# A recurrent unit's small products over four quarters of the array, its copies and elementwise steps given out anew

## The chip, the cores and the metric

The kernel runs on one core of a Trainium2 chip. The metric is device time in microseconds, the median of the runs. The engines that matter are TensorE (PE; its weight loads are PEld), VectorE (DVE), ScalarE (ACT) and GpSimd (POOL).

## The reference

One block of a network: a token mixer with two branches (softmax attention with a forget gate, and an RWKV-7 recurrence), then a gated convolutional feed-forward part. The change lies in the recurrence alone, 8 heads of 64 over 1024 tokens:

```python
def step(state, inp):
    r_t, w_t, k_t, v_t, a_t, b_t = inp
    sa = jnp.einsum('bhvk,bhk->bhv', state, a_t)
    state = state * w_t[:, :, None, :] + sa[..., None] * b_t[:, :, None, :] + v_t[..., None] * k_t[:, :, None, :]
    y_t = jnp.einsum('bhvk,bhk->bhv', state, r_t)
    return state, y_t
...
kk = heads(k * k_k)
kk = kk / jnp.maximum(jnp.sqrt(jnp.sum(kk * kk, axis=-1, keepdims=True)), L2_EPS)
k_mod = k.astype(jnp.float32) * (1 + (a - 1) * k_a)
...
mean = jnp.mean(y, axis=-1, keepdims=True)
var = jnp.mean(jnp.square(y - mean), axis=-1, keepdims=True)
y = ((y - mean) * lax.rsqrt(var + GN_EPS)).reshape(bsz, seq, RWKV_WIDTH) * ln_w + ln_b
bonus = (jnp.sum(r_h * k_h * r_k, axis=-1, keepdims=True) * v_h).reshape(bsz, seq, RWKV_WIDTH)
return ((y + bonus) * g).astype(p.dtype)
```

## The kernel before

The recurrence is computed in chunks of 64 tokens, in closed form. A *unit* is a pair of heads (`p`, four of them) and half of the tokens (`hf`), so there are eight units, numbered 0 to 7 here (`k` in the code), with eight chunks each. One head of the pair lies on partitions 0 to 63, the other on 64 to 127 (`HS[0]`, `HS[1]`).

`pre` prepares a unit. It loads two rows of `d_lora`, forms the decay (`cum`, `el`, `en`), normalises the key (`ksq`, `ssq`, `kr`) and in eight elementwise steps makes `ar` (the vectors read by), `bk` (those written with) and `rkb`, mostly on VectorE. Then come the products `p1` (`p` in the profile) of `bk` with `ar`, masked into `E`; a triangular solve of 31 steps on VectorE (`t` and `E32`, shown as `t` and `E`) on blocks that go out and back by DMA (`sm`, `M32`, `se`, `TT`); transposes `vt` and `at`, copied into `UV` and `QA`; transposes `tb`; and the product `q`.

`main` finishes a unit. VectorE transposes a quarter of `TT` into `X` (two instructions); the products `xi` and `zi` complete the inverse in `TT`. The product `uw` applies it to `QA`, and gives `Wt` and the second half of `UV`; the product `mz` of `Wt` and `E` gives `Zt` and the transition `Mt`. Both are 16 products of 64x64 by 64x128, for each chunk and head, and go into two PSUM banks of four chunks each. Head h is read from partitions `HS[h]` and written to partitions `HS[h]`. Blocks `sp` and `yp` follow, then eight steps of the state `S` (TensorE to ScalarE and back), then `y`, its mean `mu` (subtracted by the first `stt` on `y`), its variance `va` and the group norm.

Two chains, `main_chain` for unit k and `pre_chain` for the units after it, are generators. Each `yield` says how long, in the planner's nanoseconds, the chain stays away; meanwhile the planner `Weave` fills TensorE with the big products of the next projections (`qk`, `ps_rkv`, `v`, `gt`). This writes TensorE's order, which is fixed. The orders of VectorE, ScalarE, GpSimd and the queues come from a scheduler that knows the program's order and dependencies. Where `marks` holds an instruction, `add_manual_dep` without a semaphore puts another one behind it in that order: `X` stands behind the last state step `S`, the last mask `E` and, from unit 5 on, the last copy of `QA`.

Of the kernel before, what the change touches and what calls it, by code (L numbers as in the profile page):

```python
# [12 lines left out]
ALU = mybir.AluOpType  # L13
# [3 lines left out]
S = 1024  # L17
# [5 lines left out]
CH = 64  # L23
# [109 lines left out]
def hybrid_block(ctx: ExitStack, tc: tile.TileContext, a, out):  # L133
# [32 lines left out]
    def V(name, i=0, n=1):  # L166
        o, _ = VEC[name]
        return vec[:, o + i : o + i + n]
# [197 lines left out]
    with ExitStack() as es:  # L366
# [328 lines left out]
        def c3(ap):  # L695
            return ap.rearrange("p (c s) -> p c s", s=CH)
# [23 lines left out]
        def pre(k, p, hf):  # L720
# [8 lines left out]
            def chunk_tile(nm, bufs, *dims):  # L729
                return rw.tile([128, *dims], F32, tag=nm, name=f"{nm}{n}", bufs=bufs)  # L730
# [27 lines left out]
                yield 200  # L758
            ar = chunk_tile("ar", 2, 2, NCU, CH)
            stt(ar[:, 0], c3(kr), nkk[:, p : p + 1], el[:, :, 0:CH], op0=ALU.mult, op1=ALU.mult)  # L760
            stt(kr, kr, V("k_k", p), al, op0=ALU.mult, op1=ALU.mult)
            tt(bk[:, :, 0, :], c3(kr), c3(en), op=ALU.mult)
            nc.gpsimd.tensor_copy(bk[64:128, :, 2, :], bk[64:128, :, 0, :])
            tt(ar[:, 1], c3(rr), el[:, :, 1:], op=ALU.mult)
            ts(al, al, V("k_a", p), oka[:, p : p + 1], op0=ALU.mult, op1=ALU.add)
            tt(al, al, kk, op=ALU.mult)
            tt(bk[:, :, 1, :], c3(al), c3(en), op=ALU.mult)
            pcd = chunk_tile("pcd", 3, NCU)
            nc.gpsimd.tensor_copy(pcd, el[:, :, CH])
            rkb = tmp("ksq")  # L770
            stt(rkb, rr, V("r_k", p), al, op0=ALU.mult, op1=ALU.mult)
            yield 10500


            while (k - 2, 0) not in passed:
# [55 lines left out]
            for e in range(2):  # L831
                for h in range(2):
                    nc.scalar.copy(UV[HS[1 - h], e::2, h, :], v4[HS[e], :, h, :])
                    marks["QA"] = nc.vector.tensor_copy(QA[HS[h], e::2, 1, :], a4[HS[e], :, h, :])
            yield 2000
            ps = [gen(f"tb{n}{h}") for h in range(2)]
            for c in range(NCU):
# [15 lines left out]
        def main(k, p, hf):  # L853
            o = units.pop((p, hf))
            n = f"{p}_{hf}"
            cs = slice(hf * NH, hf * NH + NH)
            pcd, ar, E, QA, TT, bon, UV = (o[k] for k in ("pcd", "ar", "E", "QA", "TT", "bon", "UV"))


            X = rw.tile([128, NCU, 32], F32, tag="X", name=f"X{n}", bufs=1)  # L860
            B0 = (slice(0, 32), slice(64, 96))
            B1 = (slice(32, 64), slice(96, 128))
            yield max(0, o["ready"] - weave.now - 2500)
            for h in range(2):
                i = nc.vector.transpose(X[B0[h], :, :], TT[B0[h], :, 0:32])
                for x in ("S", "E", "bank") if k == 0 else ("S", "E", "QA") if k > 4 else ("S", "E"):
                    if x in marks:
                        tc.add_manual_dep(i.ins, marks[x].ins.name, NOSYNC)
            yield max(1300, o["ready"] - weave.now)
            xi = gen(f"xi{n}")  # L870
            for c in range(NCU):
                for h in range(2):
                    mm(xi[B1[h], c * 32 : c * 32 + 32], E[B0[h], c, h, 0, 32:64], X[B0[h], c, :], start=True, stop=True)
            for h in range(2):
                nc.scalar.copy(X[B1[h], :, :], hx(xi[B1[h], 0 : NCU * 32], 32))
            yield 2360
            zi = gen(f"zi{n}")
            for c in range(NCU):
                for h in range(2):
                    mm(zi[B0[h], c * 32 : c * 32 + 32], X[B1[h], c, :], TT[B1[h], c, 32:64], start=True, stop=True)  # L880
            for h in range(2):
                nc.scalar.copy(TT[B0[h], :, 32:64], hx(zi[B0[h], 0 : NCU * 32], 32))

            yield 2000
            Wt = rw.tile([128, NCU, CH], F32, tag="Wt", name=f"Wt{n}", bufs=1)
            for c0 in range(0, NCU, 4):
                ps = gen(f"uw{n}{c0}")
                for c in range(c0, c0 + 4):
                    for h in range(2):
                        x = (c - c0) * 128  # L890
                        mm(ps[HS[h], x : x + 128], TT[HS[h], c, :], QA[HS[h], c, :, :], start=True, stop=True)
                pv = ps.rearrange("p (c a s) -> p c a s", a=2, s=CH)
                nc.vector.tensor_copy(Wt[:, c0 : c0 + 4, :], pv[:, :, 1, :])
                for h in range(2):
                    nc.scalar.copy(UV[HS[h], c0 : c0 + 4, h, :], pv[HS[h], :, 0, :])
            yield 2970
            Zt = rw.tile([128, NCU, CH], F32, tag="Zt", name=f"Zt{n}", bufs=1)
            for c0 in range(0, NCU, 4):
                ps = gen(f"mz{n}{c0}")
                for c in range(c0, c0 + 4):  # L900
                    for h in range(2):
                        x = (c - c0) * 128
                        mm(ps[HS[h], x : x + 128], Wt[HS[h], c, :], E[HS[h], c, h, 1:3, :], start=True, stop=True)
                pv = ps.rearrange("p (c a s) -> p c a s", a=2, s=CH)
                tt(Zt[:, c0 : c0 + 4, :], pv[:, :, 0, :], ar[:, 1, c0 : c0 + 4, :], op=ALU.add)
                for h in range(2):
                    tt(Mt[HS[h], c0 : c0 + 4, HS[h]], pv[HS[h], :, 1, :],
                       ident[HS[h], HS[h]].unsqueeze(1).to_broadcast([64, 4, CH]), op=ALU.add)

            yp = py.tile([128, NCU, CH], F32, tag="yp", name=f"yp{n}")  # L910
            sp = py.tile([128, NCU, CH], F32, tag="sp", name=f"sp{n}")
            S = [state.get(p)]

            for c in range(NCU):
                for h in range(2):
                    mm(sp[HS[h], c, :], E[:, c, h, 2, :], UV[:, c, h, :], start=c == 0, stop=False, more=True)
                for h in range(2):
                    mm(yp[HS[h], c, :], UV[:, c, h, :], E[:, c, h, 1, :], start=c == 0, stop=False, more=True)
            passed.add((k, 0))
            yield 3400  # L920
            last_c = NCU - 1 - hf
            for c in range(last_c + 1):
                if S[c] is not None:
                    mm(sp[:, c, :], Mt[:, c, :], S[c], start=False, stop=c == last_c, more=True)
                S.append(rw.tile([128, CH], F32, tag="state", name=f"S{n}{c}", bufs=8))
                state_done(nc.scalar.activation(S[-1], sp[:, c, :], AF.Copy, scale=pcd[:, c : c + 1]), c == last_c)
                if c + 1 < NCU:
                    yield 1150

            for c in range(NCU):  # L930
                if S[c] is not None:
                    for h in range(2):
                        mm(yp[HS[h], c, :], S[c][HS[h], :], Zt[HS[h], c, :], start=False, stop=c == NCU - 1, more=True)
            state[p] = S[-1]
            passed.add((k, 1))

            y = rw.tile([128, NH], F32, tag="y", name=f"y{n}", bufs=1)
            nc.scalar.copy(y, yp.rearrange("p c s -> p (c s)"))

            def part(nm, i):  # L940
                return rw.tile([128, NH], F32R, tag=nm, name=f"{nm}{i}{n}", bufs=1)

            mu = gen(f"mu{n}")
            yield 700
            yield from head_sums(mu, y, part("Zt", "r"), part("Wt", "r"))
            stt(y, mu, -1.0 / CH, y, op0=ALU.mult, op1=ALU.add)
            ysq = rw.tile([128, NH], F32, tag="ysq", name=f"ysq{n}", bufs=1)
            nc.scalar.activation(ysq, y, AF.Square)
            yield 2700
            va = gen(f"va{n}")  # L950
            yield from head_sums(va, ysq, part("Zt", "s"), part("Wt", "s"))
            gg = rw.tile([128, NH], F32, tag="ysq", name=f"gg{n}", bufs=1)
            nc.sync.dma_start(gg, d_lora[2, p, :, cs])
            rs = rw.tile([128, NH], F32, tag="Zt", name=f"rs{n}", bufs=1)
            nc.scalar.activation(rs, va, AF.Ln, scale=1.0 / CH, bias=epsr[:, 1:2])
            nc.scalar.activation(rs, rs, AF.Exp, scale=-0.5)
            stt(y, y, V("ln_w", p), rs, op0=ALU.mult, op1=ALU.mult)
            stt(y, y, V("ln_b", p), bon, op0=ALU.add, op1=ALU.add)
            tt(gg, y, gg, op=ALU.mult)
            nc.sync.dma_start(d_orw[p, :, cs], gg)  # L960
# [1111 lines left out]
```

## Time and profile before

| | us |
|---|---|
| median of 3 runs | 1649.46 (1647.59 to 1650.44) |
| the profiled execution's own time | 1648.58 |
| its span in the profile | 1646.8 |
| TensorE busy | 1606.6 (98%) |
| VectorE busy | 1214.0 (74%) |
| ScalarE busy | 827.6 (50%) |

The span runs from the first to the last instruction of the program; the rest of the own time lies around it. The eight units fill about 150 to 620 us; attention, the output products and the feed-forward part follow. Busy times of TensorE overlap, since a matmul's record is longer than the distance to the next one; the distance between starts tells how long a block holds the engine.

### The profile page before, as it was taken

The page shows a single profiled execution, that of the slowest core. Times are in us where ns is not written, and L with a number is a line of the kernel's source. Part 1 is how long each engine was busy: PE and PEld are TensorE (multiplying, and loading weights), DVE is VectorE, ACT ScalarE, POOL GpSimd, SP SyncE. Part 2 cuts the span into 40 slices and gives each one's busy share as a digit, 9 for nine tenths or more (in the row PEclk, how much of TensorE's full clock was granted, in tenths as well). Part 3 has the DMA queues.
Part 4 walks back from the last instruction along what each step waited for, and adds up shares of the span by engine and source line. Part 5 has one row for each costly group of instructions (what it writes and reads, how often), then busy time and mean ns, then how long its engine had stood idle before and what let it go on. Part 6 is the DMA issues. An engine that isn't in the chain of part 4 may idle for free.

```text
span 1646.8 us, 25966 instructions
## 1 busy us (share of the span) xinstructions
PE 1606.6 (98%) x9694; PEld 1339.6 (81%) x9694; DVE 1214.0 (74%) x2345; ACT 827.6 (50%) x1557; POOL 159.2 (10%) x189
## 2 busy tenths in 40 slices
PE   7999999999999999999999999999999999999998
PEld 7777788898978788888888888788888888888886
DVE  4786787878876536888678547887777777886677
ACT  5563345444445656777623235644444444555455
POOL 0011101111111011333132000000000000000000
PEclk9999999999999999999999999999999999999999
DMA  9397645543433336434197420242232232675363
GB/s 338 121 344 229 183 130 139 137 117 94 114 103 98 97 122 163 128 106 118 50 357 264 175 80 26 84 135 96 96 120 98 96 109 96 223 256 160 122 211 109
DMA packets 121646, 240.60 MB, mean 146 GB/s; under 512 B 40048, under 2 KB 48880, under 8 KB 121520
## 3 DMA queue, kind: packets, MB, share of 16 engines
q1 hardware_dynamic: 113040, 220.58, 41.2%
q0 software_dynamic: 8480, 18.37, 4.2%
q8 instruction: 76, 1.25, 0.3%
q14 instruction: 50, 0.41, 0.1%
HBM read 173.35 MB, written 65.54 MB: 145 GB/s over the span
## 4 chain that ended last, share of the span: by engine, by line
PE 58%; DVE 5%; ACT 2%; DMA 2%; issue 1%; SPq 0%; POOL 0%; ACTq 0%; DVEq 0%; POOLq 0%
PE X L141 13%; PE D L141 13%; PE Y L141 6%; PE wo L141 5%; PE br L141 5%; PE W L141 3%; PE rk_ps L141 3%; PE gt L141 3%; PE ov L141 2%; PE lg L141 2%; PE tp L145 1%; DMA vh<-d_v 1%; DVE quads L1075 1%; DVE P L1085 1%; DVE tl L1115 0%
## 5 line engine op out<-in xcount | busy, mean ns | idle before, releaser
L141 PE MATMUL D<-op,op 128*128 128x512 f32 x924 | 209.8, 389 | 0.0
L141 PEld LDWEIGHTS D<-op,op 128*128 128x128 f32 x924 | 173.3, 188 | 36.3 <-DVE op L1295 0.3
L141 PE MATMUL X<-T_m,S 128*128 128x512 f32 x440 | 107.8, 390 | 1.7 <-ACT T_m L1756 1.1
L141 PEld LDWEIGHTS X<-T_m,S 128*128 128x128 f32 x440 | 82.4, 188 | 20.4 <-ACT T_m L1756 2.5
L1294 ACT CAST op<-g 128x512 fp32r<-128x512 f32 x77 | 47.8, 621 | 72.9 <-PE D L141 47.6
L1295 DVE TENSOR_TENSOR op<-g,op 128x512 fp32r<-128x512 f32 x77 | 53.0, 689 | 41.2 <-ACT op L1294 41.2
L1553 DVE SCALAR_TENSOR_TENSOR c<-ab,vec,c 128x512 f32<-128x512 f32 x88 | 65.9, 750 | 18.4 <-ACT c L1556 16.8
L807 DVE TENSOR_TENSOR t<-E,M 128x60 f32<-128x60 f32 (+24 forms) x248 | 55.7, 224 | 26.7 <-DMA M<-sm 20.7
L1519 DVE TENSOR_TENSOR A<-ur,A 128x512 fp32r<-128x512 f32 x64 | 44.0, 689 | 38.7 <-ACT A L1515 38.5
L1519 DVE TENSOR_TENSOR S<-ur,S 128x512 fp32r<-128x512 f32 x66 | 45.5, 691 | 35.2 <-ACT S L1515 35.0
L1515 ACT CAST S<-ur 128x512 fp32r<-128x512 f32 x66 | 41.0, 622 | 55.8 <-DVE ur L1508 30.6
L290 DVE TENSOR_TENSOR lo_in<-raw_in,hi_in 128x512 fp32r<-128x512 f32 x84 | 55.5, 701 | 15.3 <-PE gt L141 4.5
L141 PE MATMUL Y<-T_h,A 128*128 128x512 f32 x264 | 63.7, 390 | 0.3 <-ACT T_h L1756 0.3
L288 ACT CAST hi_in<-raw_in 128x1024 fp32r<-128x1024 f32 x42 | 43.9, 1050 | 40.0 <-PE qk L141 18.6
L141 PE MATMUL Y<-T_h,S 128*128 128x512 f32 x264 | 63.5, 390 | 0.4 <-ACT T_h L1774 0.4
L809 DVE TENSOR_TENSOR E<-E,t 128x60 f32<-128x60 f32 (+24 forms) x248 | 57.6, 232 | 6.3
L1115 DVE TENSOR_TENSOR tl<-tp,th 128x512 fp32r<-128x512 f32 (+1 forms) x80 | 50.0, 631 | 15.3 <-ACT th L1112 15.1
L1515 ACT CAST A<-ur 128x512 fp32r<-128x512 f32 x64 | 39.6, 621 | 42.9 <-PE X L141 31.3
L141 PE MATMUL W<-B_f,A 128*128 128x512 f32 x252 | 60.6, 389 | 0.0
L141 PE MATMUL X<-B_b,A 128*128 128x512 f32 x252 | 60.5, 389 | 0.0
L141 PEld LDWEIGHTS Y<-T_h,S 128*128 128x128 f32 x264 | 49.5, 188 | 11.0 <-ACT T_h L1774 0.8
L141 PEld LDWEIGHTS Y<-T_h,A 128*128 128x128 f32 x264 | 49.5, 188 | 11.0 <-ACT T_h L1756 0.7
(485 smaller groups left out, 4160.6 us busy)
## 6 DMA issues: line engine op xcount, KB each, us to landing
raw_in<-in_w_in SPq DMA_DIRECT2D x50, 512.0 KB, 3.7
wm<-in_w_mod SPq DMA_DIRECT2D x48, 512.0 KB, 7.4
ur<-in_w_up SPq DMA_DIRECT2D x44, 512.0 KB, 4.0
g<-d_g SPq DMA_DIRECT2D x35, 512.0 KB, 4.1
d_g<-gs SPq DMA_DIRECT2D x44, 256.0 KB, 2.1
d_g<-c SPq DMA_DIRECT2D x33, 256.0 KB, 4.5
d_st<-qh SPq DMA_DIRECT2D x64, 128.0 KB, 2.5
stA<-d_st POOLq DMA_DIRECT2D x8, 1024.0 KB, 8.1
```

What stands on the lines that cost most here:

```text
L141: nc.tensor.matmul(o, lhsT, rhs, start=start, stop=stop, skip_group_check=more)
L145: nc.tensor.transpose(o, i, eye)
L288: nc.scalar.copy(hi, raw)
L290: nc.vector.tensor_tensor(lo[:, c : c + NH], raw[:, c : c + NH], f32(hi[:, c : c + NH]), op=ALU.subtract)
L807: tt(tv, E32[:, 0:J, s : s + 1].to_broadcast([128, J, W]), M32[:, s : s + 1, s + 1 : 32].to_broadcast([128, J, W]), op=ALU.mult)
L809: tt(E32[:, 0:J, s + 1 : 32], E32[:, 0:J, s + 1 : 32], tv, op=ALU.add)
L1115: tt(tl[:, 0:w], tp[:, 0:w], f32(th[:, 0:w]), op=ALU.subtract)
L1294: nc.scalar.copy(hi, src)
L1295: tt(lo, src, f32(hi), op=ALU.subtract)
L1515: nc.scalar.copy(hi, src)
L1519: tt(lo, src, f32(hi), op=ALU.subtract)
L1553: stt(c, ab[:, x + hf * NH : x + hf * NH + NH], V("conv_w", 22 * x + i), c, op0=ALU.mult, op1=ALU.add)
```

## The change

Four things are changed.

- `uw` and `mz`: the two banks now take the even and the odd chunks. For an odd chunk head h is written to the other partition half, `HS[1 - h]`. The copies and sums that read the odd chunks take each head by itself: `Wt` and `Zt` are made by three instructions a unit each where there were two; `UV` and `Mt` keep four.
- The four copies of `at` into `QA` go from VectorE to ScalarE.
- The eight elementwise steps of `pre` were issued together, with a pause of 10500 behind them; now a pause of 800 stands between them, and one of 4900 at the end. The copy of `pcd` by GpSimd stands ahead of the last step, as before.
- For units 5 to 7, `X` stands also behind the instruction that subtracts the mean from `y` of the unit before.

```diff
--- before.py
+++ after.py
@@ pre
             stt(ar[:, 0], c3(kr), nkk[:, p : p + 1], el[:, :, 0:CH], op0=ALU.mult, op1=ALU.mult)
+            yield 800
             stt(kr, kr, V("k_k", p), al, op0=ALU.mult, op1=ALU.mult)
+            yield 800
             tt(bk[:, :, 0, :], c3(kr), c3(en), op=ALU.mult)
             nc.gpsimd.tensor_copy(bk[64:128, :, 2, :], bk[64:128, :, 0, :])
+            yield 800
             tt(ar[:, 1], c3(rr), el[:, :, 1:], op=ALU.mult)
+            yield 800
             ts(al, al, V("k_a", p), oka[:, p : p + 1], op0=ALU.mult, op1=ALU.add)
+            yield 800
             tt(al, al, kk, op=ALU.mult)
+            yield 800
             tt(bk[:, :, 1, :], c3(al), c3(en), op=ALU.mult)
+            yield 800
             pcd = chunk_tile("pcd", 3, NCU)
             nc.gpsimd.tensor_copy(pcd, el[:, :, CH])
             rkb = tmp("ksq")
             stt(rkb, rr, V("r_k", p), al, op0=ALU.mult, op1=ALU.mult)
-            yield 10500
+            yield 4900
...
                     nc.scalar.copy(UV[HS[1 - h], e::2, h, :], v4[HS[e], :, h, :])
-                    marks["QA"] = nc.vector.tensor_copy(QA[HS[h], e::2, 1, :], a4[HS[e], :, h, :])
+                    marks["QA"] = nc.scalar.copy(QA[HS[h], e::2, 1, :], a4[HS[e], :, h, :])
@@ main
-                for x in ("S", "E", "bank") if k == 0 else ("S", "E", "QA") if k > 4 else ("S", "E"):
+                for x in ("S", "E", "bank") if k == 0 else ("S", "E", "QA", "y") if k > 4 else ("S", "E"):
...
-            for c0 in range(0, NCU, 4):
-                ps = gen(f"uw{n}{c0}")
-                for c in range(c0, c0 + 4):
-                    for h in range(2):
-                        x = (c - c0) * 128
-                        mm(ps[HS[h], x : x + 128], TT[HS[h], c, :], QA[HS[h], c, :, :], start=True, stop=True)
-                pv = ps.rearrange("p (c a s) -> p c a s", a=2, s=CH)
-                nc.vector.tensor_copy(Wt[:, c0 : c0 + 4, :], pv[:, :, 1, :])
+            ps = [gen(f"uw{n}{e}") for e in range(2)]
+            for c in range(NCU):
                 for h in range(2):
-                    nc.scalar.copy(UV[HS[h], c0 : c0 + 4, h, :], pv[HS[h], :, 0, :])
+                    x = c // 2 * 128
+                    mm(ps[c % 2][HS[h ^ c % 2], x : x + 128], TT[HS[h], c, :], QA[HS[h], c, :, :], start=True, stop=True)
+            pv = [x.rearrange("p (c a s) -> p c a s", a=2, s=CH) for x in ps]
+            nc.vector.tensor_copy(Wt[:, 0::2, :], pv[0][:, :, 1, :])
+            for h in range(2):
+                nc.vector.tensor_copy(Wt[HS[h], 1::2, :], pv[1][HS[1 - h], :, 1, :])
+            for e in range(2):
+                for h in range(2):
+                    nc.scalar.copy(UV[HS[h], e::2, h, :], pv[e][HS[h ^ e], :, 0, :])
...
-            for c0 in range(0, NCU, 4):
-                ps = gen(f"mz{n}{c0}")
-                for c in range(c0, c0 + 4):
-                    for h in range(2):
-                        x = (c - c0) * 128
-                        mm(ps[HS[h], x : x + 128], Wt[HS[h], c, :], E[HS[h], c, h, 1:3, :], start=True, stop=True)
-                pv = ps.rearrange("p (c a s) -> p c a s", a=2, s=CH)
-                tt(Zt[:, c0 : c0 + 4, :], pv[:, :, 0, :], ar[:, 1, c0 : c0 + 4, :], op=ALU.add)
+            ps = [gen(f"mz{n}{e}") for e in range(2)]
+            for c in range(NCU):
                 for h in range(2):
-                    tt(Mt[HS[h], c0 : c0 + 4, HS[h]], pv[HS[h], :, 1, :],
+                    x = c // 2 * 128
+                    mm(ps[c % 2][HS[h ^ c % 2], x : x + 128], Wt[HS[h], c, :], E[HS[h], c, h, 1:3, :], start=True, stop=True)
+            pv = [x.rearrange("p (c a s) -> p c a s", a=2, s=CH) for x in ps]
+            tt(Zt[:, 0::2, :], pv[0][:, :, 0, :], ar[:, 1, 0::2, :], op=ALU.add)
+            for h in range(2):
+                tt(Zt[HS[h], 1::2, :], pv[1][HS[1 - h], :, 0, :], ar[HS[h], 1, 1::2, :], op=ALU.add)
+            for e in range(2):
+                for h in range(2):
+                    tt(Mt[HS[h], e::2, HS[h]], pv[e][HS[h ^ e], :, 1, :],
                        ident[HS[h], HS[h]].unsqueeze(1).to_broadcast([64, 4, CH]), op=ALU.add)
...
-            stt(y, mu, -1.0 / CH, y, op0=ALU.mult, op1=ALU.add)
+            marks["y"] = stt(y, mu, -1.0 / CH, y, op0=ALU.mult, op1=ALU.add)
```

The scheduled orders move with it. On TensorE, `uw` of unit 0 stood as two rows of eight, `uw_00` and `uw_04`; now pairs of `uw_00` and `uw_01` alternate. On ScalarE, what stands between unit 1's last cast and its copies of `tb` (`UV` from `vt`, `QA` from `at`) now reads:

```order
L840 COPY UV_1_1844<-vt_1_1992 64x4x64 x2
L841 COPY QA_1_1843<-at_1_1993 64x4x64 x2
L840 COPY UV_1_1844<-vt_1_1992 64x4x64
L841 COPY QA_1_1843<-at_1_1993 64x4x64
L840 COPY UV_1_1844<-vt_1_1992 64x4x64
L841 COPY QA_1_1843<-at_1_1993 64x4x64
```

Where four copies of `UV` stood alone, the four of `QA` now stand among them.

## The prediction

> **What bounds the kernel now.** I read the page's busy line first, then the sums of the stretch from 150 to 620 us, in which the eight recurrent units run and to which the whole change belongs, then TensorE's waits there.
>
> ```profile
> span 1646.8 us, 25966 instructions
> PE 1606.6 (98%) x9694; PEld 1339.6 (81%) x9694; DVE 1214.0 (74%) x2345; ACT 827.6 (50%) x1557; POOL 159.2 (10%) x189
> ...
> 150.00:620.00 470.00, 461.99 (x4226) 386.17 (x4225) 341.12 (x932) 228.04 (x431) 66.19 (x89) 1.00 0.44 125
> ```
>
> In the last row the columns are length, then busy time of TensorE, its weight loads, VectorE, ScalarE and GpSimd, then granted clock. TensorE works 462 of 470 us at clock 1.00; VectorE works 341. The waits of TensorE in that stretch (us in total, times, longest):
>
> ```profile
> PE qk L141 <- DVE ql L415: 1.9, 1, 1.9
> PE v L141 <- DVE vs L978: 1.4, 2, 0.9
> ...
> PE va L141 <- ACT Zts L712: 1.0, 1, 1.0
> PE va L141 <- POOL Wts L715: 0.9, 1, 0.9
> PE zi L141 <- ACT X L875: 0.8, 1, 0.8
> PE p L141 <- DVE bk L767: 0.4, 1, 0.4
> ```
>
> They come to a few us, so TensorE's own work sets the time, and its order is written by the planner: the big products that follow (`qk`, `ps_rkv`, `v`, `gt`) move up at once when a small product takes less. What is saved on TensorE here is saved at the end, unless another engine becomes late.
>
> **The products `uw` and `mz`.** The timeline of TensorE in unit 2 (start, us, tile, count); each product of fp32 numbers shows as two matmul records, so 16 products are x32:
>
> ```profile
> 329.56 1.96 PE L141 MATMUL uw<-QA,TT 64*64 64x128 f32 x32
> 331.45 0.74 PE L141 MATMUL v<-lo_v,u_hi 128*128 128x256 f32 x4
> ...
> 335.00 1.96 PE L141 MATMUL mz<-E,Wt 64*64 64x128 f32 x32
> 336.89 0.34 PE L141 MATMUL sp<-UV,E 128*64 128x64 f32 x4
> 337.06 0.29 PE L141 MATMUL yp<-E,UV 128*64 128x64 f32 x4
> ...
> 338.90 1.22 PE L141 MATMUL v<-hi_v,u_hi 128*128 128x256 f32 x8
> ```
>
> From start to the next start `uw` holds TensorE for 1.89 us, and so does `mz`: 0.118 us for a pair of records. Only two 64x64 quarters of the array work, the ones on the diagonal. The order of unit 1 on TensorE before (`qk` are big products):
>
> ```order
> L141 MATMUL qk_0_2824<-u_lo,hi_in_2491 128x512 x6
> L141 MATMUL uw_10_2869<-QA_1_1841,TT_1_1983 64x128 x8
> L141 MATMUL uw_14_2881<-QA_1_1841,TT_1_1983 64x128 x8
> L141 MATMUL qk_0_2824<-u_hi,lo_in_2492 128x512 x8
> L141 MATMUL qk_1_2911<-u_hi,hi_in_2491 128x512 x6
> ```
>
> Two blocks of eight, each into one bank, then the big products. Now, at the same place:
>
> ```order
> L141 MATMUL uw_10_2872<-QA_1_1843,TT_1_1985 64x128 x2
> L141 MATMUL uw_11_2873<-QA_1_1843,TT_1_1985 64x128 x2
> L141 MATMUL uw_10_2872<-QA_1_1843,TT_1_1985 64x128 x2
> L141 MATMUL uw_11_2873<-QA_1_1843,TT_1_1985 64x128 x2
> ...
> L141 MATMUL qk_0_2826<-u_hi,lo_in_2494 128x512 x7
> L141 MATMUL qk_1_2914<-u_hi,hi_in_2493 128x512 x7
> ```
>
> Even and odd chunks now alternate between two banks and, by the partitions of their outputs, between the two diagonals; 14 big products still stand between `uw` and `mz`. No row of before has all four quarters at work, so I bound it. At worst nothing overlaps: 1.89. At best the time halves: 0.95. The nearest row is the `sp`/`yp` block above: two tiles of 128 rows by 64 columns fill the array, and 64 records take from 336.89 to 338.90, 31 ns each. A quarter with 128 moving columns is half the rows and twice the columns, the same share of the array, so 32 records would take 1.00. Two row strips that write two banks also run together already, in `p`:
>
> ```profile
> 351.85 1.16 PE L141 MATMUL p<-ar,bk 64*128 64x128 f32 x16
> 352.94 0.43 PE L141 MATMUL sp<-S,Mt 128*128 128x64 f32 x2
> ```
>
> 16 records in 1.09 us, 0.136 a pair (start included). I take 1.05, one pair's 0.118 of starting up on top of the half, rounded: 0.84 saved, 16 times (two products, eight units): **-13.4 us** (bounds 0 and -15.1).
>
> The weight loads, from the groups of the same stretch (count, busy, mean ns):
>
> ```profile
> L141 PEld LDWEIGHTS p<-ar,bk 64*128 64x128 f32 x256 | 15.5, 187 | 3.9 <-issue 2.0 <-DVE bk L767 0.9 <-PE va L141 0.4
> L141 PEld LDWEIGHTS uw<-QA,TT 64*64 64x64 f32 x256 | 13.8, 133 | 2.2 <-issue 1.9
> ```
>
> A load of `p` is 54 ns longer than one of `uw`, yet a pair of `p` takes only 18 ns more, start included, so loads lie mostly under products. [...]
>
> **The elementwise work behind them.** Groups of the stretch:
>
> ```profile
> L834 DVE COPY QA<-at 64x256 f32<-64x256 f32 x32 | 13.5, 422 | 6.9 <-PE at L145 6.6
> L833 ACT COPY UV<-vt 64x256 f32<-64x256 f32 x32 | 11.7, 367 | 14.8 <-PE vt L145 14.5
> L905 DVE TENSOR_TENSOR Zt<-mz,ar 128x256 f32<-128x256 f32 x16 | 6.7, 422 | 1.0 <-PE mz L141 0.7
> L893 DVE COPY Wt<-uw 128x256 f32<-128x256 f32 x16 | 6.6, 419 | 4.8 <-PE uw L141 4.7
> ```
>
> Per unit VectorE loses four `QA` copies (1.69 us) and gains one copy for `Wt` and one sum for `Zt`, since the odd chunks' halves lie crossed (0.84): 0.85 less. I credit nothing for it, as VectorE is not the bound. ScalarE gains four copies of about 0.367, 1.5 us. Queued behind them are the copies of `tb` and the next casts; who waits first is product `q`, which reads `UV`, whose last copy is now seventh of eight. Unit 4 on ScalarE and TensorE:
>
> ```profile
> 414.45 1.50 ACT L833 COPY UV<-vt 64x256 f32<-64x256 f32 x4 [3.16 <-PE vt L145]
> ...
> 417.34 0.86 PE L141 MATMUL q<-UV,E 64*64 64x64 f32 x22
> ```
>
> `UV` would end at 415.95 + 3 x 0.367 = 417.05, still 0.3 before `q`: nothing, and at most 0.8 a unit were that cover gone.
>
> The mark that matters more is `Wt`, for which `mz` waits. VectorE's last `Wt` copy and TensorE's `mz` in units 1, 3 and 4 (the end of a copy is its start plus 0.42):
>
> ```profile
> 286.42 0.42 DVE L893 COPY Wt<-uw 128x256 f32<-128x256 f32 x1
> ...
> 287.39 0.87 PE L141 MATMUL mz<-E,Wt 64*64 64x128 f32 x12
> ...
> 381.55 0.42 DVE L893 COPY Wt<-uw 128x256 f32<-128x256 f32 x1
> ...
> 382.78 0.44 PE L141 MATMUL mz<-E,Wt 64*64 64x128 f32 x4
> ...
> 428.80 0.23 DVE L809 TENSOR_TENSOR E<-E,t 128x69 f32<-128x69 f32 x1
> 428.95 0.42 DVE L893 COPY Wt<-uw 128x256 f32<-128x256 f32 x1
> ...
> 430.34 1.96 PE L141 MATMUL mz<-E,Wt 64*64 64x128 f32 x32
> ```
>
> The margins are 0.55, 0.81 and 0.97 us. In these units VectorE runs the solve of the next unit (`t`, `E`) back to back, in a fixed order. Its order in unit 1 before:
>
> ```order
> L807 TENSOR_TENSOR t_0_2560<-E_0_2558,M_0_2553 128x68
> L893 COPY Wt_1_2868<-uw_10_2869 128x256
> L809 TENSOR_TENSOR E_0_2558<-E_0_2558,t_0_2560 128x4x17
> L807 TENSOR_TENSOR t_0_2560<-E_0_2558,M_0_2553 128x64
> L809 TENSOR_TENSOR E_0_2558<-E_0_2558,t_0_2560 128x4x16
> L893 COPY Wt_1_2868<-uw_14_2881 128x256
> ```
>
> Each copy followed its bank, two solve steps apart. Now, at the same place:
>
> ```order
> L814 TENSOR_TENSOR t_0_2563<-E_0_2561,M_0_2556 128x68
> L816 TENSOR_TENSOR E_0_2561<-E_0_2561,t_0_2563 128x4x17
> L814 TENSOR_TENSOR t_0_2563<-E_0_2561,M_0_2556 128x64
> L899 COPY Wt_1_2871<-uw_10_2872 128x4x64
> L816 TENSOR_TENSOR E_0_2561<-E_0_2561,t_0_2563 128x4x16
> L901 COPY Wt_1_2871<-uw_11_2873 64x4x64 x2
> ```
>
> The last copy stands behind the same steps and one more copy, 0.4 later, while `mz` comes 0.84 sooner. The new waits: unit 1 0.84 + 0.4 - 0.55 = 0.7; unit 3 0.4; unit 4, where one step of 0.23 also moves ahead of the last copy, 0.5; unit 2, with a margin near 1.9 but four steps moved ahead, 0.3. Together **+1.9**.
>
> **The three `X` behind `y`.** Unit 4's tail, on VectorE and then TensorE:
>
> ```profile
> 461.70 0.43 DVE L865 STREAM_TRANSPOSE X<-TT 32x256 f32<-32x256 f32 x1 [3.63 <-DMA TT<-se]
> 462.17 0.69 DVE L946 SCALAR_TENSOR_TENSOR y<-mu,y 128x512 f32<-128x512 f32 x1
> ...
> 465.19 0.50 PE L141 MATMUL va<-Zts,blk_r 128*128 128x512 f32 x1 [1.02 <-ACT Zts L712]
> 466.54 0.50 PE L141 MATMUL va<-Wts,blk_r 128*128 128x512 f32 x1 [0.85 <-POOL Wts L715]
> ```
>
> `y` stood behind `X`, which waited 3.63 us for its DMA, and `va` stood 1.0 + 0.9 for it; ScalarE, late by this, then cost `zi` 0.8 (rows above). VectorE's order there before (`E` are the masked `p`, `QA` the copies of `at`):
>
> ```order
> L787 TENSOR_TENSOR E_0_5086<-p_3_014_5144,cst_117 128x4x128
> L834 COPY QA_0_5087<-at_0_5258 64x4x64 x4
> L865 STREAM_TRANSPOSE X_1_5371<-TT_1_4618 32x256
> L946 SCALAR_TENSOR_TENSOR y_0_5140<-mu_0_5142,y_0_5140 128x512
> L865 STREAM_TRANSPOSE X_1_5371<-TT_1_4618 32x256
> ```
>
> `y` stood between the two `X`. Now, at the same place:
>
> ```order
> L794 TENSOR_TENSOR E_0_5114<-p_3_004_5158,cst_117 128x4x128
> L794 TENSOR_TENSOR E_0_5114<-p_3_014_5159,cst_117 128x4x128
> L957 SCALAR_TENSOR_TENSOR y_0_5155<-mu_0_5157,y_0_5155 128x512
> L872 STREAM_TRANSPOSE X_1_5386<-TT_1_4635 32x256 x2
> L853 COPY QA_0_5115<-q_0_5331 128x8x64
> ```
>
> `y` now goes first: **-2.7**. But unit 5's `Wt` rides on the solve, which starts on a DMA and doesn't come sooner; I give back 1.5 there. `X` queued behind `y` waits at most for `mu`, and I put 0.8 for that and all small collisions (0 to 3): **+2.3** together.
>
> **The steps given out singly.** Seven pauses of 0.8 us and 4.9 us in place of 10.5 us: the planner's sum is the same, each step keeps its instructions (DVE, two POOL copies, no DMA), and the rows around them change places only by one or two. Their reader `p` waited once, 0.4; I take 0, at most 8 x 0.4 = 3.2.
>
> **Sum** against the profiled execution's own 1648.58 us (0.88 under the median, 1.8 us of it outside the span): -13.4 + 1.9 - 2.7 + 2.3 = -11.9, so 1636.7; on the median's footing 1637.6.
>
> **Rivals.** *VectorE becomes the pace-setter* in units 0 to 5: the solve runs back to back and both products' gain is waited away there (12 x 0.84 = 10.1 us): 1649.46 - 13.4 - 2.7 + 10.1 + 0.8 = 1644.2. For it speak the margins under 1 us; against it that VectorE is free 129 of 470 us. *The array empties when the quarters change*: each `uw` record lasts 0.272 us (mean, row below) against a pace of 0.118, and at seven changes a product that adds 7 x 0.154 = 1.08 us, 16 times 17.2: 1649.46 + 17.2 - 2.7 = 1664. It makes the kernel slower from the point where a product takes more than 1.89 + (3.3 + 2.7) / 16 = 2.27 us. Against it: `sp` and `yp` change column halves with every product and run at 31 ns.
>
> ```profile
> L141 PE MATMUL uw<-QA,TT 64*64 64x128 f32 x256 | 15.7, 272 | 0.0
> ```
>
> [...] That the change does not split the work at all is excluded by the order above.
>
> **Numbers.** Forecast 72%, VectorE 15%, bare loads 6%, emptying 7%. Faster by over 0.2% (3.3 us, about what a measurement of this kernel can tell) are the first two, less a little: 86%. Same 7%, slower 7%. The range reaches from the best bound without new waits, 1649.46 - 15.1 - 2.7 = 1631.7, to the second case with some us of collisions: 1632 to 1646.5.
>
> **What would show it.** Right: `uw` and `mz` x32 near 1.05 us from start to next start; `va` in unit 4 without its two waits; short waits of `mz` for `Wt`. Wrong: a pace still near 0.118 us a pair; waits of `mz` or `q` that sum to over 6 us; `X` behind `y` that makes `xi` wait.

## The result and the profile after

The changed kernel takes 1653.97 us (median of 7 runs, 1651.48 to 1656.68) against 1647.59 for the kernel before (7 runs, 1645.79 to 1650.44): ratio 1.0038 [1.0028, 1.0048], slower by 0.4%, where 1637.6 was forecast. The bracket is a 95% interval. The profiled run of after is the slowest of its seven, so its trace shows 7.9 us more of span where the medians show 6.4. Its span, busy lines and stretch from 150 to 620 us (columns as in the prediction: length, TensorE, weight loads, VectorE, ScalarE, GpSimd, granted clock):

```profile
span 1654.7 us, 25998 instructions
PE 1602.1 (97%) x9694; PEld 1330.5 (80%) x9694; DVE 1207.4 (73%) x2329; ACT 836.8 (51%) x1589; POOL 159.4 (10%) x189
150.00:620.00 470.00, 449.40 (x4192) 370.43 (x4191) 329.70 (x912) 233.68 (x458) 63.37 (x85) 0.99 0.42 119
```

TensorE was busy 462 of the 470 us, and is now for 449. The products did become quick. The timeline of TensorE in unit 0:

```profile
235.53 1.10 PE L141 MATMUL uw<-QA,TT 64*64 64x128 f32 x32
236.56 1.90 PE L141 MATMUL ps_rkv<-u_lo,hi_in 128*128 128x512 f32 x7
```

From start to next start `uw` holds TensorE for 1.03 us; 1.89 before, 1.05 forecast. But TensorE's waits in the stretch, 7.8 us in all before, are 19.9 now. The largest, and the one that was forecast (us in total, times, longest):

```profile
PE v L141 <- DVE vs L989: 5.3, 4, 3.0
PE sp L141 <- ACT S L937: 2.9, 1, 2.9
PE qk L141 <- DVE ql L415: 2.4, 1, 2.4
PE ps_rkv L141 <- DVE gs L359: 1.6, 1, 1.6
...
PE mz L141 <- DVE Wt L899: 0.6, 1, 0.6
```

The wait of `mz` for `Wt` that was forecast is the small part: 1.0 us in the whole list, and by the starts inside its eight blocks 2.9. `v`, `qk` and `ps_rkv` are big products. They write into one of two PSUM banks (`bufs=2` in the kernel) and wait until VectorE has emptied the bank of two tiles ago (`vs`, `ql`, `gs`). A second loss stands right behind such a wait, in TensorE's clock (columns as in the first view, two stretches of after):

```profile
440.00:445.00 5.00, 2.74 (x23) 2.54 (x22) 4.92 (x12) 0.65 (x2) 0.61 (x2) 1.00 0.00 0
445.00:449.00 4.00, 3.25 (x16) 3.25 (x17) 3.90 (x12) 0.31 (x1) 0.28 (x1) 0.57 0.25 72
```

TensorE waited there for 3.0 us, and for 3.4 of the next 4 us the granted clock is one half, which costs 1.7. The units hold three such stretches after (445, 476, 548 us), one before.

I summed start-to-next-start times on TensorE from the first `ssq` to the last `va`: the small products with the waits inside a block, then of all others what exceeds a form's usual time, at half clock and outside it. The rest of the stretch is 416 to 418 us in every kernel of this table (the lower five are experiments told below):

| kernel | `uw`+`mz` | waits | half clock | stretch |
|---|---|---|---|---|
| before | 30.1 | 10.5 | 1.5 | 458.9 |
| after | 19.8 | 25.2 | 4.5 | 466.9 |
| quarters alone | 20.8 | 20.5 | 4.1 | 462.2 |
| other edits alone | 30.4 | 17.1 | 0 | 465.0 |
| quarters, VectorE's order of before | 19.8 | 25.2 | 6.3 | 467.5 |
| before, in the quarters' order | 30.1 | 10.5 | 0 | 457.2 |
| quarters, odd `Wt` by ScalarE | 17.3 | 21.5 | 1.5 | 457.0 |

So after saves 10.3 us in products and pays 14.7 in waits and 3.0 in clock. Each row is one execution, and executions of one kernel lie some us apart (those of after 5.2), so a difference of 2 or 3 us between two rows is not clear of that.

### The profile page after: what moved, and what is told of

Read it like the earlier page. It is cut to its first block, busy times and chain, and to the rows that moved or that the text cites. A ratio compares the mean times of both kernels' runs of the same rounds, so it can differ in the third digit from the quotient of the medians.

```text
span 1654.7 us, 25998 instructions
## 1 busy us (share of the span) xinstructions
PE 1602.1 (97%) x9694; PEld 1330.5 (80%) x9694; DVE 1207.4 (73%) x2329; ACT 836.8 (51%) x1589; POOL 159.4 (10%) x189
## 4 chain that ended last, share of the span: by engine, by line
PE 63%; DVE 6%; ACT 3%; DMA 2%; issue 1%; SPq 0%; DVEq 0%; ACTq 0%
PE X L141 14%; PE D L141 13%; PE Y L141 7%; PE wo L141 5%; PE gt L141 5%; PE br L141 4%; PE rk_ps L141 4%; PE W L141 3%; PE ov L141 2%; PE lg L141 2%; PE tp L145 1%; PE ps_rkv L141 1%; DVE quads L1086 1%; DVE P L1096 1%; DVE E L816 0%
```

## The experiments

All ratios are against the kernel before, timed on the same chip in five rounds.

**Which part costs.** Theory V: TensorE, quicker by the products, meets VectorE's fixed order too soon. Theory O: the other edits spoil the order. The first run is the change's hunk on `uw` and `mz` alone (two lines of it here); the second is everything else.

```diff
-                        mm(ps[HS[h], x : x + 128], TT[HS[h], c, :], QA[HS[h], c, :, :], start=True, stop=True)
+                    mm(ps[c % 2][HS[h ^ c % 2], x : x + 128], TT[HS[h], c, :], QA[HS[h], c, :, :], start=True, stop=True)
```

> Only uw and mz in the new form (four quarters); the QA copies stay on VectorE, the elementwise steps together, X without y. Both theories: uw and mz hold TensorE about 1.1 us each. Theory V (TensorE, 13 us quicker, meets VectorE's fixed order sooner and waits for evictions and for the longer Wt, Zt, Mt block): TensorE's waits in the units rise by 10 us or more here already, and the time is 1645 to 1653. Theory O (the other three edits spoilt VectorE's order): waits stay near the 8 us of before and the time is near 1637.

> Only the other edits (QA copies by ScalarE, steps singly, X behind y); uw and mz as before at 1.89 us. Theory V: little changes, 1644 to 1650, the two waits of va in unit 4 gone. Theory O: the time rises by 8 us or more, over 1655.

Quarters alone: 1650.33, ratio 1.0013 [1.0004, 1.0022]. The others alone: 1655.60, 1.0046 [1.0033, 1.0058]. Neither gains. The first shows V's picture, with products saved and waits in their place. The second, 6.6 us slower, is outside what V expected and at O's bound: each theory holds for one part. The stretch and the largest waits of the first:

```profile
150.00:620.00 470.00, 453.42 (x4211) 374.19 (x4210) 345.11 (x946) 226.72 (x428) 68.51 (x89) 0.99 0.44 123
PE v L141 <- DVE vs L982: 3.6, 2, 2.3
PE va L141 <- POOL Wts L715: 2.9, 2, 2.0
```

Two runs take one part out of after: the singly given steps, and the `QA` copies (back on VectorE).

> The changed kernel with the eight elementwise steps issued together again. Theory V: within 4 us of the changed kernel's 1654. Theory O with the singly given steps as its cause: back by 8 us or more, below 1646.

> The changed kernel with the four QA copies on VectorE again (0.42 us each, 1.7 us more on VectorE a unit). Theory V: VectorE has more to do and the time does not fall, 1653 to 1660; the waits of q for ScalarE's UV (1.5 us in all) go. Theory O with ScalarE's queue as its cause: below 1648.

Without the single steps 1652.43, 1.0019 [1.0011, 1.0028]; with `QA` on VectorE 1655.41, 1.0039 [1.0025, 1.0054]. The steps cost about 0.2% beside the rest; `QA`, beside the rest, nothing. Each of the three other edits alone:

```diff
+                for x in ("S", "E", "bank") if k == 0 else ("S", "E", "QA", "y") if k > 4 else ("S", "E"):
+            yield 800
+                    marks["QA"] = nc.scalar.copy(QA[HS[h], e::2, 1, :], a4[HS[e], :, h, :])
```

> The kernel before with X of units 5 to 7 behind y and nothing else. If the mark does what the prediction says, va's 1.9 us of waits go and the time is 1645 to 1648. If it is the cause of the other edits' loss of 6.6 us, 1653 or more.

> The kernel before with the eight elementwise steps given out singly and nothing else. If this is the cause of the other edits' loss, 1653 or more; if it is neutral as predicted, 1647 to 1651.

> The kernel before with the four QA copies by ScalarE and nothing else. The other edits together cost 6.6 us, the singly given steps alone 5.0 and the mark alone 1.6, so nothing should be left for this one: 1646 to 1650. If it costs 3 us or more, the three do not add up.

`X` behind `y`: 1649.61, 1.0010 [1.0001, 1.0019]; the two waits of `va` in unit 4 are gone as forecast, and 1.4 to 1.7 us each for `k`, `gs` and `bk` stand elsewhere. The single steps: 1653.68, 1.0031 [1.0020, 1.0043]. `QA`: 1651.81, 1.0024 [1.0015, 1.0033], though VectorE lost work. TensorE's largest wait with `QA` alone, and, below the dots, two with the steps alone:

```profile
PE tb L145 <- DVE y L946: 3.9, 1, 3.9
...
PE sp L141 <- ACT S L933: 2.4, 1, 2.4
PE qk L141 <- DVE ql L415: 2.1, 1, 2.1
```

The three add up to 0.65% where together they cost 0.46%, a gap that lies within the intervals. Each moves waits about, so I don't add single edits up.

**Does the planner's price or room help?** The planner counts a quarter product at half its columns; at four quarters 0.3 is nearer (`share`). Then two pauses were lengthened, so that more big products stand between `uw`, `mz` and what follows (2970 to 3660, 3400 to 4090).

> The quarters alone, and the planner's price of these products lowered from half to 0.3 of a full one, as they now last 1.03 us and not 1.89. The planner then puts about 0.7 us more of big products behind each block, so that the following steps come no sooner after VectorE's work than before. Theory V (the gain was lost because TensorE came to VectorE's fixed order too soon): TensorE's waits in the units fall from 17 us to near 8 and the time to 1637 to 1643. Rival theory S (the scheduler's orders of VectorE and ScalarE come out differently with every edit, and waits with them, wherever TensorE stands): within 3 us of 1650.

> The changed kernel with the same lower price. Theory V: 8 us or more below 1654. Theory S: within 4 us of 1654.

> The quarters alone at the lower planner's price, and the pauses behind uw and mz longer by what the price fell (3660 and 4090 in place of 2970 and 3400), so that the planner puts 0.69 us more of big products there; the run before this one did not move any, as the chain was shortened with the price. Theory V (TensorE comes to fixed latencies of VectorE and DMA too soon): waits of TensorE in the units fall from 17 to 8 to 11 us and the work moved into the units is missing behind them: 1637 to 1643. Theory S (orders come out differently, wherever TensorE stands): 1647 or more.

> The changed kernel with the same price and the same longer pauses. Theory V: 8 us or more below the changed kernel's 1654. Theory S: within 4 us of it.

Price: 1650.34, 1.0017 [1.0008, 1.0025], and with all edits 1654.07, 1.0041 [1.0029, 1.0053]; in the first only 74 of TensorE's 9694 records changed places, so nothing was tested. Room: 1676.77, 1.0174 [1.0160, 1.0187], and 1679.68, 1.0195 [1.0181, 1.0209]. It drew about 100 big products out of the later stage into the units. The units grew by 34.7 us against quarters alone, and what follows them shrank by only 7.0. The largest wait in the units became another:

```profile
PE xi L141 <- DVE X L865: 6.8, 2, 4.9
```

V's forecast of 1637 to 1643 is missed. But with so much work moved these runs speak against adding room, and hardly for or against V.

**Is it the order?** TensorE's order is the planner's, and is the same in before and in the quarters' kernel; VectorE's is written by the scheduler: 104 of the 2361 rows in the quarters' trace have no partner in the order of before (the 32 new half-width ones among them; counts of rows below are of this kind). Theory S: that new order is the loss.

> Only the four-quarter form of uw and mz, but each of its products issued twice, so that a block lasts 2.06 us where it lasted 1.89 before and 1.03 in the quarter form. The order of all engines is that of the quarter form. Theory V (TensorE, 13 us quicker, reaches its fixed order's meeting points with VectorE too soon): the waits between the first ssq and the last va fall back from 16.6 us to 8 to 11, and the time is before + 16 x 0.17 = before + 2.7, some 1650 to 1652. Theory S (every edit reshuffles the fixed orders, and before's happens to be a good one): the waits stay near 16 to 17, the products cost 16 x 1.03 more than in the quarter form, and the time is near 1666.

> The four-quarter form in uw alone (mz as before): 8 x 0.86 = 6.9 us less of products. If the loss sits where mz follows uw too soon (mz for Wt, v and qk behind it), half of it is there: waits 8 + 4 = 12, time before - 2. Theory V with the whole gain eaten: within 1.5 us of before. Theory S: waits 4 to 10 us over before's 8, without relation to the 6.9, time anywhere from before - 3 to before + 3.

> The four-quarter form, with VectorE relieved: for the blocks of input and weights that are loaded while the units run, the low part (input minus its rounded copy, one VectorE subtraction of about 1.3 us each) is left out, and the high part stands in its place, so TensorE's products are as many as before. To be read against the run that leaves the same out of the kernel before. Theory V: with VectorE earlier by what it no longer does, the quarters bring 8 to 13 us against that run. Theory S, or waits that hang on DMA and not on VectorE: the two are within 3 us.

> The kernel before without the same low parts, the control of the run with quarters. Its waits from the first ssq to the last va are 8 us now, a few of them on VectorE: both theories expect 0 to 5 us less than before, 1643 to 1648.

Each product issued twice: 1669.98, 1.0131 [1.0118, 1.0144]. It looks like S, but the run is inconclusive: against my assumption the scheduler moved 218 rows of VectorE again. Quarters in `uw` alone: 1650.49, 1.0014 [1.0005, 1.0022]: `uw` took 6.9 us less, all of it eaten, 2.5 of it inside `mz`. The next two leave the low parts out and serve for timing alone: quarters 1649.10, 1.0008 [0.9999, 1.0016], the control 1654.23, 1.0036 [1.0024, 1.0048]. The quarters are 5.1 us quicker than their control, between what V (8 to 13) and S (under 3) expected. But VectorE had less to do in the control than in the kernel before, and it grew 5.6 us slower, which neither theory expected. TensorE's order is that of before there (528 records read a high part in place of a low one), while 482 of VectorE's 2269 rows stand elsewhere, and the trace has 6.8 us at half clock in the units. So an order written anew can cost some us by itself, and the pair, whose two orders of VectorE differ too, doesn't isolate VectorE's load.

The next two hold the order. A list of places ties each instruction of VectorE and ScalarE in the units to the one that shall stand ahead of it, without a wait:

```diff
+        for x, y in zip(order, order[1:]):
+            tc.add_manual_dep(own[y], own[x].name, NOSYNC)
```

> The four-quarter form of uw and mz (the first experiment's kernel), with the rows of VectorE and ScalarE in the stretch of the units held to the order of the kernel before; the one copy and one sum more per unit stand right behind their neighbours. TensorE's order is that of the kernel before anyway. Theory S (the order that the scheduler writes anew for VectorE is what costs): the waits fall back to 8 to 11 us, PE busy stays near 452 of 470, and the time is before - 13.8 + 2 to 5 for Wt and the meeting points, some 1637 to 1640. Theory V (TensorE, quicker, comes too soon whatever the order): the waits stay at 15 to 17, the time within 2 us of the first experiment's, some 1649 to 1651.

> The kernel before (uw and mz on two quarters), with the rows of VectorE and ScalarE in the stretch of the units held to the order that the scheduler wrote for the four-quarter form. Theory S: 5 to 9 us of waits more than before although no product is quicker, some 1654 to 1658. Theory V: before's time within 2 us, 1647 to 1650, since TensorE comes as late as before.

Quick products in the old order: 1658.43, 1.0059 [1.0045, 1.0073]. Slow products in the new order: 1648.08, 0.9994 [0.9986, 1.0003]. For the quarters S falls: the new order is no worse for the slow products, and the old one is worse for the quick ones. V's number for the first (1649 to 1651) is missed too. The stretch of the first and of the second:

```profile
150.00:620.00 470.00, 448.05 (x4187) 370.11 (x4187) 344.14 (x943) 222.24 (x422) 65.81 (x85) 0.99 0.42 119
```

```profile
150.00:620.00 470.00, 461.86 (x4228) 385.39 (x4226) 339.12 (x930) 229.08 (x433) 66.85 (x89) 1.00 0.45 125
```

In one order, quicker products alone should not make the end later, so something was added. Half clock is one part, 6.3 us here and 1.5 before (table). For another, VectorE in unit 0, before (start, us, line):

```profile
236.87 0.42 DVE L893 COPY Wt<-uw 128x256 f32<-128x256 f32 x1
...
237.87 0.42 DVE L893 COPY Wt<-uw 128x256 f32<-128x256 f32 x1
...
243.09 0.43 DVE L905 TENSOR_TENSOR Zt<-mz,ar 128x256 f32<-128x256 f32 x1
...
249.47 0.75 DVE L389 SCALAR_TENSOR_TENSOR k<-ps_rkv,omu,sh_rkv 128x512 f32<-128x512 f32 x1
```

and with quick products in that same order:

```profile
238.04 0.42 DVE L892 COPY Wt<-uw 128x256 f32<-128x256 f32 x1
...
239.16 0.88 DVE L894 COPY Wt<-uw 64x256 f32<-64x256 f32 x2
...
244.83 0.85 DVE L908 TENSOR_TENSOR Zt<-mz,ar 64x256 f32<-64x256 f32 x2
...
251.66 0.74 DVE L389 SCALAR_TENSOR_TENSOR k<-ps_rkv,omu,sh_rkv 128x512 f32<-128x512 f32 x1
```

Where one copy took 0.42 us, two now take 0.88, and the sum of `Zt` the same. No row between has idle time ahead of it: VectorE runs the solve without a pause. It was 1.17 us late at the first `Wt`, and is 2.19 late at `k`. Only the last 1.0 of this is the edit's. The solve had begun 1.17 us later already, on a DMA, before any quick product ran (`uw` of unit 0 is the first). Before:

```profile
226.22 0.19 DVE L807 TENSOR_TENSOR t<-E,M 128x31 f32<-128x31 f32 x1 [0.80 <-DMA M<-sm]
```

and in this run:

```profile
227.39 0.19 DVE L807 TENSOR_TENSOR t<-E,M 128x31 f32<-128x31 f32 x1 [1.78 <-DMA M<-sm]
```

TensorE is 1.2 us early at `k`. (It was 1.6 early ahead of `uw`, since the trace of before has its half-clock stretch at 192 us; the 1.7 that `uw` and `mz` then save are lost to waits within `mz` and ahead of it.) It waits for `k` and then runs six big records at half clock:

```profile
252.45 0.97 PE L141 MATMUL ps_rkv<-u_hi,hi_in 128*128 128x512 f32 x2 [2.88 <-DVE k L389]
253.22 0.52 PE L141 MATMUL sp<-S,Mt 128*128 128x64 f32 x2
253.50 2.87 PE L141 MATMUL ps_rkv<-u_hi,hi_in 128*128 128x512 f32 x6
```

Before, the same six records:

```profile
251.25 1.63 PE L141 MATMUL ps_rkv<-u_hi,hi_in 128*128 128x512 f32 x6
```

So the unit shows what the edit adds to VectorE, not how much of the wait is the edit's. That the solves leave VectorE little room could be read before the prediction, had I asked stage by stage. Before, in eight stretches around the solves:

```profile
180.00:222.00 42.00, 40.13 (x234) 32.17 (x233) 36.20 (x104) 16.46 (x26) 4.89 (x7) 0.96 0.57 155
222.00:258.00 36.00, 36.00 (x334) 29.57 (x332) 29.75 (x98) 13.03 (x25) 2.41 (x7) 1.00 0.49 136
270.00:306.00 36.00, 36.00 (x334) 29.46 (x333) 33.45 (x100) 16.06 (x32) 4.20 (x8) 1.00 0.58 149
316.00:350.00 34.00, 33.53 (x412) 31.21 (x409) 31.33 (x99) 14.48 (x32) 4.49 (x8) 1.00 0.33 102
366.00:398.00 32.00, 32.00 (x304) 26.17 (x303) 28.23 (x95) 15.94 (x29) 3.83 (x6) 1.00 0.35 106
420.00:456.00 36.00, 35.07 (x410) 32.64 (x409) 33.08 (x100) 13.31 (x31) 4.90 (x8) 1.00 0.37 111
466.00:498.00 32.00, 30.54 (x296) 24.90 (x297) 28.25 (x91) 17.86 (x34) 2.57 (x5) 1.00 0.30 98
526.00:550.00 24.00, 22.97 (x251) 19.48 (x251) 18.88 (x76) 12.74 (x27) 0.00 (x0) 1.00 0.17 52
```

VectorE, the third busy time, takes 79 to 93% of them, 239 of 272 us together. **Theory W**: the 0.85 us that the quarter form adds to VectorE in each unit is what eats the gain. The last run takes it away, with every other row held in the quarters' order:

```diff
-                nc.vector.tensor_copy(Wt[HS[h], 1::2, :], pv[1][HS[1 - h], :, 1, :])
+                nc.scalar.copy(Wt[HS[h], 1::2, :], pv[1][HS[1 - h], :, 1, :])
```

> The first experiment's kernel with one edit: the two copies of the odd chunks' halves of Wt are made by ScalarE, ahead of its UV copies, in place of VectorE. VectorE then has as many instructions as before (one copy less for Wt, one sum more for Zt); all other rows of VectorE, ScalarE and TensorE stay in the first experiment's order. Theory W (VectorE runs without a pause through the solves of units 0 to 4, so the 0.85 us that the quarter form adds to it in each unit pushes everything behind it back, and the waits and half-clock windows follow from that): VectorE is no later than in the crosswise run with slow products, TensorE keeps at least the products' gain of units 5 to 7 (6 x 0.86 = 5.2), waits 8 to 12 us, some 1641 to 1645. Theory V alone (TensorE comes too soon, the added instructions don't matter): waits stay near 16, 1649 to 1651.

1647.47, ratio 0.9997 [0.9988, 1.0006], between the two theories. The stretch, and its largest waits:

```profile
150.00:620.00 470.00, 452.69 (x4232) 374.00 (x4230) 339.25 (x932) 234.05 (x448) 68.92 (x89) 1.00 0.45 126
PE va L141 <- POOL Wts L715: 3.3, 2, 2.4
PE v L141 <- DVE vs L982: 2.6, 2, 2.2
PE qk L141 <- DVE ql L415: 1.8, 1, 1.8
```

Against quarters alone the stretch is 5.2 us shorter (462.2 to 457.0): two half-clock stretches fewer (2.6), and 3.5 less inside `uw` and `mz`. The other waits rose by 1.0. That is W's part, some 2.6 us in the ratios (0.16%, with intervals that overlap). But against the slow products in nearly the same order (30.1 + 10.5 in the table) TensorE saves 12.8 us and waits 11.0 more, and loses 1.5 at half clock: 457.2 and 457.0. VectorE's own rows hardly come sooner either: the second `X` of unit 6 starts at 501.66 and 503.65, `gs` in unit 7 at 584.70 and 585.41, where this run was 1.1 us behind at 149 us, before any quick product. So V holds for the rest, also without the added instructions: in one order, with as much for VectorE to do, quick and slow products end together, and TensorE's gain is waited away. Which link of the chain sets that pace isn't shown: in the last run VectorE itself waits in the stretch 50 us for DMA, 36 for ScalarE and 32 for TensorE.

## Why the prediction was wrong

- **The products** (-13.4): right. 1.03 us each, 16 x 0.86 = -13.8 where nothing waits inside a block. The four quarters run together: 32 records in 1.03 us, where two quarters took 1.89 before. Loads don't stand bare (given 6%): the block's eight steps of four records take 0.13 us each, and one load alone lasts 0.133 here too, which would leave nothing for the products. Nor does the array empty (7%), which by the prediction's estimate added 1.08 us a product, more than a whole block took.
- **The step that failed** is "What is saved on TensorE here is saved at the end, unless another engine becomes late", and its ground, "VectorE is not the bound". I took VectorE's 341 of 470 us, an average over stages; around the solves it works 79 to 93% of the time, and quick and slow products in one order end together (457.0 and 457.2). By terms: the waits inside `uw` and `mz`, forecast at +1.9, came to 3.3 (19.8 over 16 x 1.03; 2.9 of it in `mz`). The terms for everything else, -2.7 and +2.3, measured 14.7 more of waits. Half clock, which the sum did not have, cost 3.0 beside it in the traces.
- **The rival that came nearest** is VectorE as the pace-setter (1644.2). Its mechanism, a gain that is waited away, is what the crosswise runs and the last run show, though they don't show VectorE's own work to be the only cause. Its price was too low: I let it eat 12 of 16 products' gain, and all is eaten; I priced neither the half-clock stretches nor that the quarter form adds 0.85 us to VectorE where it has little room. I had netted these against the `QA` copies, which lie elsewhere in the unit.
- **The singly given steps** (0, bound 3.2): wrong. Alone they cost 1.0031, some 5 us. Seven short pauses with the old sum still moved 1247 of TensorE's 9694 records and 155 of VectorE's 2345 rows; "only by one or two" was wrong. Which of these makes the cost was not separated.
- **`X` behind `y`** (-2.7): right in place, as both waits of `va` went, and worth nothing at the end (alone 1.0010).
- **`QA` by ScalarE** (0 to 0.8 a unit): nothing beside the other edits, but alone 1.0024. Its trace shows the wait of `tb` for `y` above, 3.9 us, and 6.8 us at half clock that begin inside it and cost some 2.7; TensorE's order was that of before, while 57 of VectorE's rows had moved.
- Of the signs of being wrong that I named, waits of `mz` or `q` of over 6 us did not come; that sign watched the wrong products.

## What to carry to other kernels

Ask for busy time by stage before an engine is called free: an engine at 73% over a stretch can be at up to 93% in the very part that a change touches, as VectorE here, and instructions added there delay what is queued behind them (by 1.0 us in unit 0). Where engines in fixed orders hand work back and forth, as here, a saving on the busiest one can turn wholly into lost time (here 12.8 us saved, 11.0 more waited, 1.5 at half clock): ask what the others will have ready by then. Where a scheduler writes an order anew at each edit, hold the order and exchange one thing at a time: here that crossed pair told more than all the runs before it.

## What was not expected of the hardware

After waits of 1.6 to 3.0 us TensorE's clock fell to one half for 3.41 us, at a cost of up to 1.7 us, and from within the 3.9 us with `QA` alone for 6.8. Not each such wait does it. One in after, then one before:

```profile
190.66 2.11 PE L141 MATMUL qk<-u_hi,hi_in 128*128 128x512 f32 x8 [2.44 <-DVE ql L415]
...
190.68 3.05 PE L141 MATMUL qk<-u_hi,hi_in 128*128 128x512 f32 x8 [1.87 <-DVE ql L415]
```

The longer one left the clock alone; behind the shorter one 191.6 to 195.0 us ran at half clock. In each of the twenty traces all half-clock stretches start whole multiples of 3.41 us apart, as if on a fixed grid. The 1.87 us lie inside one step of this grid (188.2 to 191.6); the 2.44 are cut by an edge at 189.4 into 1.2 and 1.3. Counted over all traces between 150 and 1630 us, for steps at full clock: with under 1 us without a matmul none of 8423 was followed by half clock, with 1 to 2 us 22 of 161, with 2 us or more all 27.

In the kernel before, a step without a matmul for 1.87 of its 3.41 us was thus enough, and this wait cost close to twice itself: 1.87 us, and up to 1.7 more at half clock behind it.
